# Two late tiles of the expert mixer are selected, and their gathers emitted, earlier in the dense stage

## The chip, the cores and the metric

The kernel runs on one core of one Trainium2 chip. The metric is device microseconds of one execution. Three runs of the kernel before gave 3964.43, 3979.69 and 3978.75 us, a median of 3978.75 us. One further execution was profiled. All times of stages and instructions below come from that one.

## The reference

The reference is one layer of a hybrid decoder: a norm, a joint input projection for two head groups, an output projection, the expert channel mixer, a per-layer input embedding and a final norm. It works on 1024 prompt rows and 64 sample rows of 1024 features. The change lies in the expert mixer, which in the reference reads:

```python
def peer(xn, wq, keys, u_tab, v_tab):
    ...
        q = (xb @ wq).reshape(PEER_BLOCK, PEER_HEADS, 2, PEER_DKEY // 2)
        s = jnp.einsum('phcd,hcnd->phcn', q, keys).astype(jnp.float32)
        sv, si = lax.top_k(s, PEER_TOPK)
        cand = sv[:, :, 0, :, None] + sv[:, :, 1, None, :]
        cv, ci = lax.top_k(cand.reshape(PEER_BLOCK, PEER_HEADS, PEER_TOPK * PEER_TOPK), PEER_TOPK)
        e = ...
        gsm = jax.nn.softmax(cv, axis=-1)
        hval = jnp.einsum('pd,phkd->phk', xb, u_tab[e])
        act = (jax.nn.gelu(hval.astype(jnp.float32), approximate=False) * gsm).astype(xb.dtype)
        return jnp.einsum('phk,phkd->pd', act, v_tab[e])
```

Each row picks 128 of 16384 experts (8 heads, 16 each), takes the product of its features with 128 rows of `u_tab`, and sums 128 weighted rows of `v_tab`.

## The kernel before

The rows are nine tiles: 0 to 7 hold 128 prompt rows each, tile 8 the 64 sample rows. The mixer is computed in two ways.

**Gathered tiles.** Tiles 0, 1, 8 (`E0`, during earlier stages) and 2, 3 (`G1`, the late tiles) fetch their own expert rows. `gather` issues 128 indirect DMAs of 128 x 1024 floats for `u_tab` and 128 more for `v_tab` on the queue of GpSimd (POOL). VectorE (DVE) works each one off with one `scalar_tensor_tensor`. Five buffers `grow` turn round, so the sixth DMA waits until DVE has used the first row. The two late tiles make 512 gathers.

**Dense tiles.** Tiles 4 to 7 (`G2`) are computed together against all experts, in 128 blocks of 128 experts:

- `hidden` multiplies one block of `u_tab` with the 512 rows (24 matmuls `ph`, since operands are split in a high and a low part: `uh` on ScalarE (ACT), `ul` on POOL).
- `gates` turns a tile's selection into weights for every expert and row. A tile takes 32 steps. A step is two comparisons `oh` on DVE, four scalings of `oh` on ACT, four matmuls `pwt` on TensorE (PE) and one copy `wst` on ACT. Ahead of its first step a tile's indices are transposed by three matmuls `pit`. After 16 steps four DMAs write the weights to `wd` in device memory.
- `act` reads weights back (`wt`), multiplies, and splits (`ah`, `al`). `dense` multiplies the result with `v_tab` (`py`, 24 matmuls a block; `vh` on ACT, `vl` on POOL).

Three stages follow one another. **Stage 1** (lines 1492 to 1513) loops over the four dense tiles and one last pass: top-k of a tile (DVE, some on POOL), the gate steps of the tile before, and a fifth of the first 96 `hidden` blocks, stored in `gd`. `TK1` says behind which pass a late tile's top-k and its whole gather are emitted. **Stage 2** (`dense_fused`) computes the last 32 blocks with `hidden` and `py` in turn; it needs every tile's weights. **Stage 3** (`dense_stored`) does `py` for the 96 stored blocks in groups of five, eight steps a group, and splits the weights of the embedding (`pga`, `pgb`, `pgx`) on the side. Then `ple` finishes all tiles, the late ones last.

The code emits the work in this order, but the framework's scheduler decides what each engine's queue holds: it orders the instructions of each engine by emission, readiness and its own clock. Each engine then runs its queue strictly in order. A gather that waits for a buffer on POOL so holds up an `ul` or `vl` behind it.

Of the kernel before, what the change touches and what calls it, by code (L numbers as in the profile page):

```python
# [166 lines left out]
PG = 0  # L167
PWS = 4
NPRE = 96
NF = 4  # L170
TK1 = {2: 1, 3: 4}
GEB = 2
GHB = 2
WQ = 32
# [5 lines left out]
G1 = [2, 3]  # L180
# [19 lines left out]
def spans(tiles):  # L200

    e = [sum(SIZE[t] for t in tiles[:i]) for i in range(len(tiles) + 1)]
    return dict(zip(tiles, e)), e[-1]
# [8 lines left out]
class K:  # L212
# [1204 lines left out]
    def build(self):  # L1417
        PS = bass.MemoryType.PSUM
        run = lambda g: [None for _ in g]
        sb = lambda name, es, **kw: self.pool(name, es=es, reuse_waits="tile", **kw)  # L1420
        with self.es:
            self.setup()
            em, ee, eg, et, ew, ex, ep, e0, e1, e2 = (ExitStack() for _ in range(10))
            acc = self.acc = self.pool("psumg", space=PS, es=eg, reuse_waits="tile")
            self.psums("psum", ep, a=2, b=3, d=1)
            self.rowed = set()
            pools = self.a_pool(e1, "1")
            mix = []

            def mixes():  # L1430
                self.setup_mix(em)
                mix.append(self.first_mix(e0))

            a = self.group_a(pools, A0, "b", mixes)
            while next(a) != "rw":
                pass
            m = mix[0]
            self.interleave(m, 1, a, IA)
            a = self.group_a(pools, A1, "b")
            self.interleave(m, IB, a, 1)  # L1440
            e1.close()
            e0.close()
            self.ep0 = ep0 = sb("early", ee, side="right")
            self.layout(ep0, [("V", [128, D], F32, ER), ("W", [128, D], F32, 1), ("xy", [128, D], F32, 1), ("Wq", [128, D], F32, 1), ("xT", [128, D], F32, 1)])
            early = self.behind(self.early(ep0), PE_)
            co = self.co = sb("co", ew, side="right")
            a = self.group_a(self.a_pool(e2, "2"), A2, "b")
            for _ in self.c_rows(co, E0[0]):
                next(a, None)
            for _ in a:  # L1450
                for _ in range(IE):
                    next(early, None)
            e2.close()
            late = self.group_b(BORDER, early)
            em.close()
            cq = sb("cq", ew, bufs=2, side="right")
            parts = [G1, G2]
            self.layout(cq, [(f"ss{g[0]}", [128, len(g), 2, 128], F32, 1) for g in parts] +
                        [(f"qT{g[0]}", [128, spans(g)[1]], F32, 1) for g in parts])
            cn = sb("cn", ew, side="right")  # L1460
            c1 = sb("cx1", ew, side="right")
            x1 = self.rows_of(c1, G1)
            cx = sb("cx2", ex)
            x = self.rows_of(cx, G2)
            da = sb("dna", eg, bufs=2)
            self.layout(da, [("uh", [128, 8, 128], F32R, DW), ("ul", [128, 8, 128], F32R, DW), ("uraw", [128, 8, 128], F32, UB)])
            tp = sb("tk", et)
            self.e12 = {}
            n3 = spans(G2[:-1])[1]
            query = self.c_query(cq, da, [(G1, x1), (G2, x)])  # L1470

            def rest():
                for t in late[:-1]:
                    yield from self.c_rows(co, t, CRING)

            run(self.rows_in(cn, G1, x1))
            run(rest())
            last = self.c_rows(co, late[-1], CRING, da, [y[:, :, n3:] for y in x])
            next(last)
            for _ in self.rows_in(cn, G2[:-1], x):  # L1480
                next(last, None)
            run(last)
            run(query)
            run(early)
            ew.close()
            ee.close()
            ep.close()
            self.group(G2)
            self.wd = self.dp.tile([self.ntok // 64, 128, 128, 64], F32, name="wd")
            self.gd = self.dp.tile([128, 128, self.ntok], F32, name="gd")  # L1490
            gp = sb("gat", eg, side="right")
            with ExitStack() as e:
                self.psums("psumw", e, i=1, w=2)
                self.psh = self.pool("psumh", bufs=3, space=PS, es=e, reuse_waits="tile")
                gw = sb("gw", e, side="right")
                self.layout(gw, [("oh0", [128, 4, 128], F32, 2), ("oh1", [128, 4, 128], F32, 2), ("it", [128, 128], F32, 2)])
                gh = sb("gh", e, bufs=2, side="right")
                gate = iter(())
                nh = 0
                for i, t in enumerate(G2 + [None]):  # L1500
                    tk = self.topk(tp, t) if t is not None else iter(())
                    while True:
                        a, b = next(tk, "end"), next(gate, "end")
                        if a == "end" and b == "end":
                            break
                    while nh < NPRE * (i + 1) // (len(G2) + 1):
                        self.nc.scalar.dma_start(self.gd[nh], self.hidden(da, gh, x, nh))
                        nh += 1
                    gate = self.gates(gw, t) if t is not None else gate
                    for t in G1:  # L1510
                        if i == TK1[t]:
                            run(self.topk(tp, t))
                            run(self.behind(self.gather(gp, t, acc=acc), PG))
            et.close()
            self.first = True
            with ExitStack() as e:
                dl = sb("dl", e, bufs=2)
                yT = sb("dy", e, side="right").tile([128, 8, self.ntok], F32, name="yT")
                with ExitStack() as e2:
                    self.ps2 = self.pool("psumy", bufs=3, space=PS, es=e2, reuse_waits="tile")  # L1520
                    self.psh = self.pool("psumh2", bufs=3, space=PS, es=e2, reuse_waits="tile")
                    dr = sb("dr", e2, bufs=2, side="right")
                    self.dense_fused(dl, dr, da, x, yT)
                    self.dense_stored(dl, dr, yT, self.ple_weights(cx, da, dl))
                self.psums("psum3", e, a=2, p=2)
                self.pst = self.pool("psumt", bufs=1, space=PS, es=e, reuse_waits="tile")
                self.ple(dl, sb("plt", e, bufs=2, side="right"), yT)
            eg.close()
            ex.close()
# [14 lines left out]
```

## Time and profile before

The profiled execution took 3954.93 us; its span, first to last instruction, is 3953.2 us. Engines run side by side, so busy times of different engines do not add up. In the page's groups a line stands with its engine, operation, output and input, count, busy time and mean.

| what | number |
|---|---|
| median of three runs | 3978.75 us |
| profiled execution, and its span | 3954.93 us, 3953.2 us |
| busy PE, DVE, POOL, ACT | 3349.9, 2957.2, 2322.7, 1222.2 us |
| moved by DMA | 1107.20 MB, of it 604.05 MB by gathers |
| first `ph` of stage 1 | 2093.9 us |
| first DVE instruction of the dense tiles' top-k | 2104.7 us |
| transposes `pit` of the last dense tile (7) | 2662.6 us |
| last `pwt` of tile 7 | about 2771 us |
| first gather of the late tiles | after 2358.7 us, where `eid` of tile 2 is written |

### The profile page before, as it was taken

To read this page: it belongs to the slowest core of one execution; us is meant where nothing else is said; L and a number is where in the kernel's file an instruction comes from. 1 tells how busy PE (TensorE), PEld (TensorE's weight loads), DVE (VectorE), ACT (ScalarE), POOL (GpSimd) and SP (SyncE) were. 2 spreads that over 40 slices of the span, in tenths; PEclk is the share of its full clock that TensorE was granted. 3 is DMA by queue.
4 is the path that set the end of the run, shared out by engine and by line. 5 is a ranking of instruction groups with operands and counts; after the bars stand their busy time and mean duration, and the time that the engine had idled before them with its cause. 6 is when DMAs were issued, how large, how long until landed. Compare 5 with 4: busy or idle time off the path is not lost. (4 is left out here: it accounts for less than half of the span.)

```text
span 3953.2 us, 52689 instructions
## 1 busy us (share of the span) xinstructions
PE 3349.9 (85%) x17749; PEld 2755.0 (70%) x17749; DVE 2957.2 (75%) x5764; ACT 1222.2 (31%) x2247; POOL 2322.7 (59%) x2051
## 2 busy tenths in 40 slices
PE   7789994865788585886699899999999989899989
PEld 7688993643566473665598677888788766677767
DVE  4454388978858879888857999986577777787775
ACT  4232221010022011111232466778332333333322
POOL 5253176555416656565544557775788777787740
PEclk9799995655698556887799999999999999999999
DMA  7266458989946998889974459888999999999962
GB/s 251 69 225 215 157 195 319 310 293 301 322 133 230 381 355 254 303 294 373 395 279 149 135 172 335 300 323 338 364 342 338 331 355 352 365 366 348 343 221 71
DMA packets 473864, 1107.20 MB, mean 280 GB/s; under 512 B 74555, under 2 KB 191545, under 8 KB 467642
## 3 DMA queue, kind: packets, MB, share of 16 engines
q0 software_dynamic: 165888, 604.05, 41.9%
q1 hardware_dynamic: 245694, 393.26, 30.7%
q10 hardware_dynamic: 62012, 106.52, 7.2%
q8 instruction: 141, 2.31, 0.2%
q14 instruction: 129, 1.06, 0.1%
HBM read 997.17 MB, written 106.43 MB: 279 GB/s over the span
## 5 line engine op out<-in xcount | busy, mean ns | idle before, releaser
L1127 POOL DMA_INDIRECT grow<-in_pv,eid x576 | 561.7, 975 | 382.9 <-DVE gacc L1155 221.6
L1127 POOL DMA_INDIRECT grow<-in_pu,eid x576 | 561.7, 975 | 343.9 <-DVE grow L1141 220.3
L1155 DVE SCALAR_TENSOR_TENSOR gacc<-grow,ac,gacc 128x1024 f32<-128x1024 f32 x571 | 732.4, 1283 | 36.8 <-DMA grow<-in_pv,eid 29.5
L1141 DVE SCALAR_TENSOR_TENSOR grow<-grow,gacc 128x1024 f32<-128x1024 f32 x576 | 686.7, 1212 | 63.5 <-DMA grow<-in_pu,eid 61.5
L1295 PE MATMUL py<-ah,vl 128*128 128x512 f32 x1024 | 410.1, 404 | 37.0 <-POOL vl L301 37.0
L1295 PE MATMUL py<-ah,vh 128*128 128x512 f32 x1024 | 407.0, 399 | 13.4 <-ACT vh L297 13.3
L326 PE MATMUL ph<-cx,uh 128*128 128x512 f32 x1024 | 408.2, 399 | 7.6 <-ACT uh L297 7.6
L328 PE MATMUL ph<-cx,ul 128*128 128x512 f32 x1024 | 407.5, 398 | 3.2 <-POOL ul L301 3.2
L1295 PE MATMUL py<-al,vh 128*128 128x512 f32 x1024 | 406.3, 397 | 0.0
L327 PE MATMUL ph<-cx,uh 128*128 128x512 f32 x1024 | 406.1, 397 | 0.0
L301 POOL TENSOR_TENSOR ul<-uraw,uh 128x1024 fp32r<-128x1024 f32 x128 | 308.2, 2409 | 152.8 <-ACT uh L297 150.8
L301 POOL TENSOR_TENSOR vl<-vraw,vh 128x640 fp32r<-128x640 f32 (+2 forms) x224 | 325.7, 1457 | 54.4 <-ACT vh L297 50.6
L297 ACT ACTIVATE vh<-vraw 128x640 fp32r<-128x640 f32 (+2 forms) x224 | 154.6, 692 | 382.7 <-PE py L1295 221.9
L1295 PEld LDWEIGHTS py<-ah,vl 128*128 128x128 f32 x1024 | 194.2, 190 | 102.6 <-POOL vl L301 60.9
L1299 DVE TENSOR_TENSOR yT<-yT,py 128x512 f32<-128x512 f32 x216 | 147.5, 684 | 143.7 <-PE py L1295 143.3
L1295 PEld LDWEIGHTS py<-ah,vh 128*128 128x128 f32 x1024 | 195.3, 191 | 65.9 <-ACT vh L297 24.7
L326 PEld LDWEIGHTS ph<-cx,uh 128*128 128x128 f32 x1024 | 195.5, 191 | 47.1 <-ACT uh L297 8.4
L328 PEld LDWEIGHTS ph<-cx,ul 128*128 128x128 f32 x1024 | 195.4, 191 | 43.9 <-POOL ul L301 4.3
L1295 PEld LDWEIGHTS py<-al,vh 128*128 128x128 f32 x1024 | 194.7, 190 | 44.4
L327 PEld LDWEIGHTS ph<-cx,uh 128*128 128x128 f32 x1024 | 195.4, 191 | 39.7
L1243 ACT ACTIVATE oh<-oh,it 128x128 f32<-128x128 f32 x512 | 161.8, 390 | 107.0 <-DVE oh L1241 96.2
L1241 DVE TENSOR_TENSOR oh<-csta,pit 128x512 f32<-128x512 f32 x256 | 161.5, 677 | 41.9 <-PE pwt L1246 41.9
(400 smaller groups left out, 7722.6 us busy)
## 6 DMA issues: line engine op xcount, KB each, us to landing
uraw<-in_puT SPq DMA_DIRECT2D x128, 512.0 KB, 4.5
vraw<-in_pvd SPq DMA_DIRECT2D x152, 320.0 KB, 5.8
cw<-in_w_out SPq DMA_DIRECT2D x128, 256.0 KB, 5.2
wd<-wst ACTq DMA_DIRECT2D x32, 1024.0 KB, 16.1
wt<-wd SPq DMA_DIRECT2D x64, 512.0 KB, 7.6
wraw<-in_w_ret SPq DMA_DIRECT2D x48, 512.0 KB, 4.9
ewq<-in_wq SPq DMA_DIRECT2D x48, 512.0 KB, 6.6
gd<-geh ACTq DMA_DIRECT2D x96, 256.0 KB, 4.5
```

The source lines that it names most:

```text
L297: nc.scalar.activation(hi, src, AF.Copy)
L301: nc.gpsimd.tensor_tensor(lo, src, hi.bitcast(F32), op=OP.subtract)
L326: mm(out, lh(k), rh(k), start=first and k == 0, stop=False)
L327: mm(out, lh(k), rl(k), start=False, stop=False)
L328: mm(out, ll(k), rh(k), start=False, stop=last and k == nk - 1)
L1127: nc.gpsimd.indirect_dma_start(out=g, out_offset=None, in_=src, in_offset=bass.IndirectOffsetOnAxis(ap=self.eid[t][:, j:j + 1], axis=0))
L1141: nc.vector.scalar_tensor_tensor(g[:, c], g[:, c], 1.0, x[:, c], op0=OP.mult, op1=OP.mult, accum_out=hv[:, i, j:j + 1])
L1155: nc.vector.scalar_tensor_tensor(y[:, c], g[:, c], ac[:, j:j + 1], y[:, c], op0=OP.mult, op1=OP.add)
L1241: nc.vector.tensor_tensor(oh[j], io, p[:, j, s + b:s + b + 4, None].to_broadcast([128, 4, 128]), op=OP.is_equal)
L1243: nc.scalar.activation(oh[0][:, j], oh[0][:, j], AF.Copy, scale=it[:, s + b + j:s + b + j + 1])
L1295: nc.tensor.matmul(p, lh[:, b, :], rh, start=b == 0 and j == 0, stop=b == nb - 1 and j == 2)
L1299: nc.vector.tensor_tensor(yT[:, d, :], yT[:, d, :], p, op=OP.add)
```

## The change

`TK1` goes from `{2: 1, 3: 4}` to `{2: -1, 3: 2}`: tile 2 is selected and its gather emitted ahead of the loop over the dense tiles (before: behind the second pass), tile 3 behind the third pass (before: behind the last). For the new place the two lines become an inner function.

```diff
-TK1 = {2: 1, 3: 4}
+TK1 = {2: -1, 3: 2}
...
+                def late_gather(i):
+                    for t in G1:
+                        if i == TK1[t]:
+                            run(self.topk(tp, t))
+                            run(self.behind(self.gather(gp, t, acc=acc), PG))
+
+                late_gather(-1)
                 for i, t in enumerate(G2 + [None]):
...
-                    for t in G1:
-                        if i == TK1[t]:
-                            run(self.topk(tp, t))
-                            run(self.behind(self.gather(gp, t, acc=acc), PG))
+                    late_gather(i)
```

No instruction of the computation is added or taken away; the queues are ordered differently. Counted over the queues from stage 1 on (a block is 24 matmuls, a gather one indirect DMA of the 512):

| place in the queue | before | changed |
|---|---|---|
| PE: blocks `ph` ahead of the `pit` of tiles 4, 5, 6, 7 | 19, 38.8, 58.8, 76 | 33.2, 60.5, 80.7, 98.1 |
| PE: blocks `ph` ahead of the last `pwt` of tile 7 | 89 | 99 |
| DVE: gathers ahead of the copy `it` of tile 7 (all six top-k done in both) | 91 | 181 |
| POOL: gathers ahead of the 64th `vl` (last of stage 2) | 286 | 359 |
| POOL: gathers ahead of the 144th `vl` (80 steps of stage 3) | 407 | 482 |
| POOL: the 512th gather stands behind | the last `vl` (224th) | the 167th `vl` |

PE, at the end of tile 7's gate steps. Each row is one or several matmuls: `pwt` of a gate step, `ph` of a hidden block, `py` of stage 2. Before:

```order
L328 MATMUL ph<-cx_13025,ul 128x512
L1246 MATMUL pwt<-oh_21886,oh_21887 128x128 x2
L326 MATMUL ph<-cx_13025,uh 128x512
L1246 MATMUL pwt<-oh_21886,oh_21887 128x128 x2
L327 MATMUL ph<-cx_13026,uh 128x512
L1246 MATMUL pwt<-oh_21900,oh_21901 128x128 x4
L328 MATMUL ph<-cx_13025,ul 128x512
```

The same place in the changed program:

```order
L1246 MATMUL pwt<-oh_22826,oh_22827 128x128 x4
L1246 MATMUL pwt<-oh_22840,oh_22841 128x128 x4
L1246 MATMUL pwt<-oh_22854,oh_22855 128x128 x4
L1246 MATMUL pwt<-oh_22868,oh_22869 128x128 x4
L1295 MATMUL py<-ah,vh 128x512 x2
L326 MATMUL ph<-cx_13025,uh 128x512
```

Before, the gate steps of tile 7 stand among 13 hidden blocks, and 9 more blocks follow ahead of the first `py`. Now 31 of the 32 steps stand in one piece, with no block between them, and the first `py` comes right behind them.

POOL, at the same place of the changed program (`ul` of the 103rd and 104th block, `vl` for stage 2, gathers of tile 2's `in_pv`):

```order
L301 TENSOR_TENSOR ul<-uraw,uh 128x1024
L1127 DMA grow<-in_pv,eid_67 128x1024 x20
L301 TENSOR_TENSOR vl<-vraw,vh 128x512 x2
L1127 DMA grow<-in_pv,eid_67 128x1024 x9
L301 TENSOR_TENSOR ul<-uraw,uh 128x1024
```

Before, one to three gathers stand between two splits there; now a run of 20 stands ahead of the first `vl` and 9 behind it.

POOL, at the end of stage 3 (the last `vl` of the stored blocks, and `nrs` of the embedding). Before:

```order
L301 TENSOR_TENSOR vl<-vraw,vh 128x128 x2
L1127 DMA grow<-in_pv,eid_68 128x1024 x2
L301 TENSOR_TENSOR vl<-vraw,vh 128x128 x3
L1127 DMA grow<-in_pv,eid_68 128x1024 x7
L291 TENSOR_SCALAR nrs<-nssq 128x1
```

The changed program:

```order
L301 TENSOR_TENSOR vl<-vraw,vh 128x640
L1127 DMA grow<-in_pv,eid_68 128x1024 x2
L301 TENSOR_TENSOR vl<-vraw,vh 128x640 x49
L301 TENSOR_TENSOR vl<-vraw,vh 128x128 x8
L291 TENSOR_SCALAR nrs<-nssq 128x1
```

Before, gathers stand between the splits up to the end, and ten stand behind the last one; now the last 57 splits have no gather among them or behind them.

## The prediction

> **What bounds the kernel now.** I read the page first, for the engines' totals:
>
> ```profile
> PE 3349.9 (85%) x17749; PEld 2755.0 (70%) x17749; DVE 2957.2 (75%) x5764; ACT 1222.2 (31%) x2247; POOL 2322.7 (59%) x2051
> q0 software_dynamic: 165888, 604.05, 41.9%
> L1127 POOL DMA_INDIRECT grow<-in_pv,eid x576 | 561.7, 975 | 382.9 <-DVE gacc L1155 221.6
> L1141 DVE SCALAR_TENSOR_TENSOR grow<-grow,gacc 128x1024 f32<-128x1024 f32 x576 | 686.7, 1212 | 63.5 <-DMA grow<-in_pu,eid 61.5
> ```
>
> PE is busiest, but the mean hides the stages. A gather moves 604.05 MB / 1152 = 0.524 MB and costs DVE 1.2 us. Next I cut the time from stage 1 on at points of the timeline (first block; first and last `pit`; last `pwt`; first `py`; first `py` of stage 3; half of it; its short last group; start of `ple`), and asked the windows view for busy times. The columns are PE, weight load, DVE, ACT, POOL, granted clock, DMA share, GB/s; the three rows below them are POOL's gathers alone in stage 3.
>
> ```profile
> 2094.00:2213.00 119.00, 105.46 (x458) 86.50 (x456) 106.34 (x582) 31.02 (x39) 60.47 (x41) 0.95 0.48 157
> 2213.00:2662.60 449.60, 421.54 (x2147) 355.40 (x2147) 415.50 (x1147) 307.41 (x609) 311.39 (x219) 0.96 0.73 260
> 2662.60:2771.00 108.40, 103.40 (x569) 89.36 (x568) 77.32 (x130) 84.57 (x185) 59.39 (x45) 0.98 0.90 336
> 2771.00:2832.00 61.00, 53.05 (x220) 42.95 (x220) 28.53 (x29) 16.96 (x23) 42.19 (x31) 0.92 1.01 380
> 2832.00:3178.00 346.00, 342.97 (x1490) 279.05 (x1489) 259.36 (x306) 111.38 (x171) 284.28 (x234) 1.00 0.97 340
> 3178.00:3508.00 330.00, 291.85 (x1159) 220.59 (x1160) 248.92 (x395) 118.51 (x193) 259.65 (x216) 0.96 1.01 357
> 3508.00:3774.00 266.00, 258.88 (x1105) 205.60 (x1104) 209.91 (x249) 97.28 (x156) 201.09 (x163) 1.00 0.98 344
> 3774.00:3805.00 31.00, 12.90 (x52) 8.39 (x50) 23.73 (x27) 4.45 (x12) 18.65 (x25) 0.78 0.96 339
> ```
>
> ```profile
> 3178.00:3508.00 330.00, 112.09 (x118) 0.96 1.01 357
> 3508.00:3774.00 266.00, 84.74 (x89) 1.00 0.98 344
> 3774.00:3805.00 31.00, 13.95 (x14) 0.78 0.96 339
> ```
>
> Stage 1 (2094 to 2771) is held by PE and DVE together: up to the last `pit` both are over 90% busy, while DMA has room (0.48, 0.73). Stage 2 is PE alone (343 of 346 us). Stage 3 is DMA and POOL in its first half (DMA share 1.01, PE 292 of 330 us), nearly PE in its second. PE's own waits there say through whom DMA works:
>
> ```profile
> PE py L1295 <- POOL vl L301: 35.0, 40, 2.0
> PE py L1295 <- ACT vh L297: 11.6, 21, 4.1
> ```
>
> The `vl` that PE waits for stand behind gathers in POOL's queue. So the idea of the change has ground: gathers leave a crowded stage for one with DMA to spare. What it costs is the order in stage 1.
>
> **The change part by part.** No work is added, so each term is a shift of PE idle time. The unit is a block of 24 matmuls, from the chain of waits in stage 2:
>
> ```profile
> 2969.97 5.53 PE py L1295 x24
> ```
>
> *(a) Later arrival at tile 7's gate steps.* PE's queue now holds 98.1 blocks ahead of tile 7's `pit`, before 76. That is 22.1 x 5.53 = **+122 us**; the 384 other `pwt` stand ahead of it in both. DVE gives a second estimate: 181 gathers instead of 91 ahead of its copy `it`, 90 x 1.21 = +109 us, all else equal. Both engines were over 90% busy, so neither shift finds a hole; I take the larger. If they add in part it is up to 25 us more. Ahead of it tile 2's top-k stands in front of tile 4's, but 14 more blocks now cover that wait. Tile 2's first gathers fall ahead of 2358.7 us, where no late gather ran before, and SP's block loads pass nothing that waits longer.
>
> *(b) The gate steps run bare.* Before, tile 7's 32 steps took 108.4 us (third row of the table) with 13 blocks between them. Now one block stands at their start and 31 steps follow alone. PE takes 1.78 us for two steps (first row, the chain of waits), so ACT sets the pace (three rows of ACT's timeline):
>
> ```profile
> 2762.37 1.78 PE pwt L1246 x16
> ```
>
> ```profile
> 2712.13 1.28 ACT L1243 ACTIVATE oh<-oh,it 128x128 f32<-128x128 f32 x4
> 2713.30 1.13 ACT L1247 ACTIVATE wst<-pwt 128x512 f32<-128x512 f32 x1
> 2714.19 1.26 ACT L1243 ACTIVATE oh<-oh,it 128x128 f32<-128x128 f32 x4
> ```
>
> From one group of scalings to the next are 2714.19 - 2712.13 = 2.06 us. 31 steps are 64 us, the block 5: 69 us, or **-39 us** against 108.4. The other end: if steps keep their old pace of 108.4 / 32 = 3.4 us, 31 take 105 us and the term is about 0.
>
> *(c) Nothing covers the weights' way through memory.* Ahead of the first `py` the last half tile of weights must be written, read back, multiplied and split. The rows are from the chain of waits, the DMA view of 2760 to 2840, and the groups of 2771 to 2900:
>
> ```profile
> 2774.46 19.04 DMA wd<-wst
> ```
>
> ```profile
> wt<-wd SPq DMA_DIRECT2D x3, 512.0 KB, 11.1
> ```
>
> ```profile
> L1274 DVE TENSOR_TENSOR ph<-ph,wt 128x512 f32<-128x512 f32 x9 | 6.3, 698 | 12.4 <-ACT ph L1263 12.3
> L297 ACT ACTIVATE ah<-ph 128x512 fp32r<-128x512 f32 x9 | 5.4, 596 | 5.4 <-DVE ph L1274 5.4
> ```
>
> The write lands at 2793.5, 22.5 us behind the last `pwt` (2771). The read takes 11.1, multiply and split 1.3: 35 us. Before, nine blocks hid it all but 61 - 53 = 8 us. Now `py` comes right behind `pwt`, and PE waits it out. It then starts slowly, as it did after a pause of a few us:
>
> ```profile
> 2800.00:2804.00 4.00, 2.60 (x5) 0.50 1.09 378
> 2804.00:2808.00 4.00, 4.00 (x11) 0.50 1.04 399
> ```
>
> Seven us at half clock lose 3.5. The term is 35 + 3.5 - 8 = **+30 us**. With the page's medians (wd 16.1, wt 7.6) it is 18; with ten us more in a crowd of gathers, 40.
>
> ```profile
> wd<-wst ACTq DMA_DIRECT2D x32, 1024.0 KB, 16.1
> wt<-wd SPq DMA_DIRECT2D x64, 512.0 KB, 7.6
> ```
>
> The Trainium skill, page "TensorE: Matmul & The Clock Gate", section "HAM oscillation — how this bites in real kernels", asks for no PE pause longer than about 3.4 us, and so speaks against this change. The two rows at 0.50 agree for the restart. Were its half clock to hold through the bare steps too, `pwt` would take twice 0.89 us a step and still hide behind ACT; chained behind it, the sum comes out as in the rival "slow steps" below.
>
> *(d) Blocks in hand.* At the last `pwt` 99 blocks are done, before 89: 10 x 5.53 = **-55 us** in what is left of stage 2, which is PE alone and has the same gathers as before.
>
> Stages 1 and 2 together: 122 - 39 + 30 - 55 = +58 us.
>
> *(e) Stage 3.* POOL has 153 gathers left at its start, before 226. But the queue fixes where they stand: in the first 80 steps 123 gathers, before 121, so this half stays at 330 us and loses some 3 us (2 x 0.524 MB at 357 GB/s). In the next 24 steps the density is as before. Only the last 48 full steps and the short group are free. The second half's 72 full steps took 266 us, 3.69 each; PE's 15 matmuls need 15/24 x 5.53 = 3.46, so 48 steps give back 11 us at most: **-11 us** (the other end 0). So nearly all of the relief falls where PE had little to wait for.
>
> *(f) The tail.* The short group and the wait for `ple` took 31 us with PE busy 12.9:
>
> ```profile
> 3805.11 1.11 PE L320 MATMUL ntr<-csta,njunk 128*128 128x128 f32 x4 [14.65 <-DVE njunk L311]
> ```
>
> Gathers between its splits slow the group (16 us for eight steps; I take 8), and DVE's last gathers stand ahead of `ple`'s first addition (of the wait of 14.65 I take off 6). **-14 us**; ends -5 and -20.
>
> The sum is 58 + 3 - 11 - 14 = **+36 us**. On the profiled execution's 3954.93 us that is 3991 us. That execution lies 0.6% under the median of 3978.75 us, so I add to the median: **4015 us**, slower by 0.9%. A measurement of this kernel can tell about 0.5%, 20 us, from no change.
>
> **The rivals.**
>
> *Slow steps.* The bare steps take 3.4 us instead of 2.06: DVE's comparisons share its queue with 19 gathers there, each of which can wait for its DMA, and PE, mostly idle, runs at half clock. For: steps in before did take 3.4. Against: then ACT and PE had blocks to work on. Sum +36 + 36 = +72 us, 4051 us.
>
> *A wash.* DVE's 109 us is the true shift of (a), the weights' way takes the page's medians (term 18): 109 - 39 + 18 - 55 = +33, and stage 3 with its tail gives back 22. Sum +11, 3990 us. For: PE's 449.6 us ahead of `pit` held some 28 us of idle time. Against: DVE had no more of it.
>
> *DMA relief in full, the other side: faster.* If stage 3 is paced by bytes as a whole, not by the place of each gather in POOL's queue, 73 fewer gathers (38 MB at 351 GB/s, 109 us) count up to PE's floor: 2304 matmuls are 96 x 5.53 = 531 us, with 13 us for the tail 544 instead of 627, -83. Sum 58 - 83 = -25, 3954 us. It decides if the first 80 steps take under 280 us instead of 330. For: the DMA share of 1.01. Against: the same 123 gathers stand between the same 80 `vl`. The Trainium skill, page "DMA: Bandwidth & Descriptors", section "Issuing engines are not separate DMA queues", says that transfers of SP, ACT and POOL share the same 16 DMA engines, whoever issues them; by that alone, the bytes taken out would come back as time. The shares of 0.97 to 1.01 with gathers and loads together agree.
>
> *The change does nothing it says.* The first gathers could be held by something else in stage 1. The queue speaks against it: the late tile's index is written ahead of tile 4's. 3979 us.
>
> **How the numbers follow.** Forecast 0.41, slow steps 0.22, a wash 0.25, faster 0.10, no effect 0.02. Slower by over 0.5%: slow steps 0.22 and most of the forecast 0.36, in all 0.58. Faster by over 0.5%: the last rival and the edge of the wash, 0.12. The rest, 0.30, lies within. The range takes in the wash with its low ends (about -20, 3960 us) and slow steps with ten us more for the weights' way and some for (a) (+85, 4064 us); it leaves out the faster rival and the far upper edge.
>
> **What would show it.** In the changed profile: tile 7's `pit` near 2662.6 + 122 = 2785 us, not before 2770 (a); 31 steps of `pwt` without `ph`, over 64 to 105 us, PE about 40% busy (b); a PE pause near 35 us that ends with `wt` and `ah`, clock 0.50 behind it (c); stage 3 beginning near 3178 + 58 = 3236 us; 80 steps in about 330 us, then steps near 3.5 us with no wait for `vl` (e); a pause ahead of `ple` under 10 us (f). I am wrong if `pit` comes by 2740, if blocks fill the gate steps after all, or if the first 80 steps fall to 280 us.

## The result, and the profile after

The changed kernel takes **4013.29 us** (median of four runs, 4010.9 to 4024.18). The kernel before takes 3972.6 us beside it (median of four runs, 3964.43 to 3979.69). The ratio is 1.0111, with a 95% interval of 1.009 to 1.0132: slower by 1.1%, 40.7 us. Forecast were 4015 us and +36 us. The total was hit more closely than the terms deserve: the base of 3978.75 us lay 6 us above this median, and the difference came out 5 us larger than forecast.

The profiled execution of the changed kernel took 4024.18 us (span 4022.4), 69 us more than that of before. Half of this is no effect of the change: the first `ph` of stage 1 comes at 2128.9 us, before at 2093.9, and the queues up to there are the same. Over all profiled executions of this study it came between 2093.9 and 2129.7 us, in no order by kernel. So all times below are counted from each execution's own first `ph`; "+" marks them. By this count the program ends at +1893.5 us, before at +1859.3: **34.2 us** later. The medians say 40.7; the 6.5 us between the two belong to no stage that I could find.

The totals on the page of the changed kernel:

```profile
PE 3387.4 (84%) x17749; PEld 2788.9 (69%) x17749; DVE 2978.6 (74%) x5764; ACT 1226.4 (30%) x2247; POOL 2327.8 (58%) x2051
q0 software_dynamic: 165888, 604.05, 41.6%
L1141 DVE SCALAR_TENSOR_TENSOR grow<-grow,gacc 128x1024 f32<-128x1024 f32 x576 | 684.9, 1212 | 37.0 <-DMA grow<-in_pu,eid 26.7
L1295 PE MATMUL py<-ah,vh 128*128 128x512 f32 x1024 | 407.2, 398 | 38.6 <-ACT ah L297 25.9
```

Counts and bytes are the old ones, and so are the means of a gather's work. PE's busy time is 37.5 us more for the same 17749 instructions, but 29.2 of it lie ahead of the first `ph` (1650.2 us against 1621.0), where the change does nothing. From there on it is 8 us. The last row has a new wait, 25.9 us for `ah`.

The timeline of the changed kernel, cut at the same points as before (first block; last `pit`; last `pwt`; first `py`; first `py` of stage 3; 80 steps; 24 steps; last full step; start of `ple`), in the windows view. Columns are PE, weight load, DVE, ACT, POOL, granted clock, DMA share, GB/s. The cuts at 80 and 104 steps lie up to 4 us late. The second fence has POOL's gathers alone, in the stretches of stage 3.

```profile
2129.00:2820.20 691.20, 648.25 (x3138) 539.57 (x3136) 649.50 (x1855) 375.70 (x694) 518.06 (x373) 0.98 0.83 290
2820.20:2901.50 81.30, 54.14 (x280) 48.53 (x277) 67.21 (x88) 68.45 (x163) 25.78 (x25) 0.80 0.77 286
2901.50:2927.70 26.20, 0.29 (x3) 0.03 (x1) 12.46 (x12) 2.86 (x5) 9.07 (x9) 0.50 0.92 340
2927.70:3271.20 343.50, 338.30 (x1464) 275.68 (x1464) 262.54 (x389) 108.05 (x167) 281.42 (x236) 0.99 0.98 349
3271.20:3607.20 336.00, 301.67 (x1216) 229.87 (x1217) 261.14 (x330) 124.29 (x201) 270.63 (x225) 0.97 1.02 367
3607.20:3690.20 83.00, 82.00 (x352) 65.26 (x351) 66.24 (x80) 32.05 (x52) 62.45 (x51) 1.00 1.01 355
3690.20:3857.20 167.00, 166.37 (x717) 133.79 (x716) 68.85 (x102) 61.43 (x98) 74.01 (x48) 1.00 0.55 164
3857.20:3874.60 17.40, 6.87 (x34) 5.02 (x32) 9.46 (x13) 4.07 (x11) 4.02 (x9) 0.76 0.71 233
```

```profile
3271.20:3607.20 336.00, 117.60 (x124) 0.97 1.02 367
3607.20:3690.20 83.00, 25.64 (x27) 1.00 1.01 355
3690.20:3857.20 167.00, 0.00 (x0) 1.00 0.55 164
```

Four things are to be seen. Stage 1 is as full as before but 122 us longer up to tile 7's `pit` (first row). Then PE is busy two thirds of 81 us, at a clock of 0.80, and not at all for 26 us. Stage 3's first 80 steps keep their gathers (124 in that row, at a DMA share of 1.02) and take nearly as long as before. And where the gathers are gone, DMA has room (share 0.55, 164 GB/s) beside a PE that is busy 166.37 of 167 us and has nothing to gain from it.

| stage | before | changed | difference |
|---|---|---|---|
| first `ph` to the last `pit` of tile 7 | 568.7 | 691.1 | +122.4 |
| to the last `pwt` | 108.5 | 81.3 | -27.2 |
| to the first `py` | 61.2 | 26.4 | -34.8 |
| to the first `py` of stage 3 | 348.5 | 343.5 | -5.0 |
| to the end of the last full step of stage 3 | 597.5 | 586.0 | -11.5 |
| to the first `ntr` of `ple` | 26.8 | 17.4 | -9.4 |
| to the end | 148.1 | 147.8 | -0.3 |

Before, the last full step ends at 3778.4 us. The prediction's table cuts at 3774, 18 matmuls earlier, and so counts 4 us of full steps as tail.

### The profile page after: what moved, and what is told of

It reads as the page before. It is cut to its first block, busy times and chain, and to the rows that moved or that the text cites. A ratio compares the mean times of both kernels' runs of the same rounds, so it can differ in the third digit from the quotient of the medians.

```text
span 4022.4 us, 52688 instructions
## 1 busy us (share of the span) xinstructions
PE 3387.4 (84%) x17749; PEld 2788.9 (69%) x17749; DVE 2978.6 (74%) x5764; ACT 1226.4 (30%) x2247; POOL 2327.8 (58%) x2051
## 4 chain that ended last, share of the span: by engine, by line
PE 30%; DVE 14%; DMA 5%; issue 4%; POOL 4%; ACT 2%; ACTq 0%; another core or an unknown queue 0%; POOLq 0%; DVEq 0%; SPq 0%
PE py L1295 13%; DVE grow L1141 3%; PE ph L326 2%; PE ph L328 2%; PE ph L327 2%; POOL grow L1127 1%; PE pwt L1246 1%; POOL vl L301 1%; DVE oh L1241 1%; DVE eq L1082 1%; DMA vraw<-in_pvd 1%; DVE gacc L1155 1%; PE pq L326 1%; PE pq L327 1%; PE pq L328 1%
## 5 line engine op out<-in xcount | busy, mean ns | idle before, releaser
L1155 DVE SCALAR_TENSOR_TENSOR gacc<-grow,ac,gacc 128x1024 f32<-128x1024 f32 x571 | 732.8, 1283 | 38.2 <-DMA grow<-in_pv,eid 30.5
L1295 PE MATMUL py<-ah,vh 128*128 128x512 f32 x1024 | 407.2, 398 | 38.6 <-ACT ah L297 25.9
L1295 PEld LDWEIGHTS py<-ah,vh 128*128 128x128 f32 x1024 | 194.8, 190 | 88.9 <-ACT ah L297 26.2
L297 ACT ACTIVATE uh<-uraw 128x1024 fp32r<-128x1024 f32 x128 | 135.4, 1058 | 276.5 <-DMA uraw<-in_puT 124.2
L1246 PE MATMUL pwt<-oh,oh 128*128 128x128 f32 x1024 | 155.7, 304 | 53.8 <-ACT oh L1243 45.8
```

The costliest lines, as they stand in the source:

```text
L297: nc.scalar.activation(hi, src, AF.Copy)
L1155: nc.vector.scalar_tensor_tensor(y[:, c], g[:, c], ac[:, j:j + 1], y[:, c], op0=OP.mult, op1=OP.add)
L1246: nc.tensor.matmul(pw[:, j, :], oh[1][:, j, :], oh[0][:, j, :], start=True, stop=True)
L1295: nc.tensor.matmul(p, lh[:, b, :], rh, start=b == 0 and j == 0, stop=b == nb - 1 and j == 2)
```

## The experiments

Their expectations name these theories. **Q** (the prediction's own): PE's queue loses blocks to the front of stage 1, so tile 7's gate steps and the weights' way through memory run bare. **T3**: tile 3's place does it. **C**: the moved gathers crowd stage 1, whatever blocks remain. **B**: stage 3's first 80 steps are paced by the bytes that stand between them; **W**: only by where a `vl` stands behind a gather.

One row for each run; the times come from its profile, counted from its first `ph`.

| run | blocks ahead of `pit` | `pit` | last `pwt` | first `py` | end | ratio (95%) |
|---|---|---|---|---|---|---|
| before | 76 | 568.7 | 677.2 | 738.4 | 1859.3 | |
| the change | 98.1 | 691.1 | 772.4 | 798.8 | 1893.5 | 1.0111 (1.009 to 1.0132) |
| tile 2 moved alone | 96 | 676.7 | 759.8 | 786.0 | 1882.6 | 1.0074 (1.0045 to 1.0104) |
| tile 3 moved alone | 76.2 | 569.3 | 681.5 | 741.2 | 1860.5 | 1.001 (0.9994 to 1.0026) |
| the change, 112 blocks | 97.8 | 690.3 | 809.8 | 838.8 | 1858.7 | 0.9989 (0.9972 to 1.0006) |
| before, 112 blocks | 88 | 631.6 | 741.4 | 824.2 | 1858.4 | 1.0000 (0.9982 to 1.0019) |
| tile 2 behind the first pass | 82.2 | 599.2 | 722.2 | 752.5 | 1861.0 | 0.9999 (0.9979 to 1.0018) |
| the change, side work spread | 98.1 | 689.0 | 768.9 | 795.2 | 1885.5 | 1.0061 (1.004 to 1.0081) |
| before, side work spread | 76 | 567.3 | 676.5 | 737.4 | 1853.4 | 0.9989 (0.9971 to 1.0006) |
| the change, 112 blocks, spread | 97.8 | 689.1 | 809.4 | 837.9 | 1869.4 | 1.0026 (1.0006 to 1.0045) |
| the change, 104 blocks | 97.8 | 688.7 | 796.6 | 823.4 | 1872.0 | 1.0034 (1.0017 to 1.0051) |
| tile 2 behind the first pass, spread | 82.2 | 598.7 | 721.5 | 751.6 | 1860.9 | 1.0008 (0.9996 to 1.002) |
| the same, 104 blocks | 83 | 602.3 | 718.1 | 787.9 | 1856.5 | 0.9983 (0.9968 to 0.9998) |

**Which half of the change?** Tile 2 alone, and tile 3 alone:

```diff
-TK1 = {2: -1, 3: 2}
+TK1 = {2: -1, 3: 4}
```

> Tile 2 moved as in the change, tile 3 where it was before (TK1 2: -1, 3: 4). Theory Q (queue): the loss comes from tile 2's gathers in stage 1, which delay tile 7's gate steps until PE's 99 blocks are used up; then 31 steps and the weights' way stand bare. PE's queue here has 96 blocks ahead of tile 7's pit and 99 ahead of its last pwt and of the first py, nearly as in the change: ratio to before 1.008 to 1.013, a pause of 25 us or more ahead of the first py. Rival T3: it is tile 3's top-k and gather behind the third pass that cost; then the ratio is 0.997 to 1.003.

```diff
-TK1 = {2: -1, 3: 2}
+TK1 = {2: 1, 3: 2}
```

> Tile 3 moved as in the change, tile 2 where it was before (TK1 2: 1, 3: 2). Q: PE's queue is that of before (76 blocks ahead of tile 7's pit, 90 ahead of its last pwt), so nothing changes: ratio 0.997 to 1.003. Rival T3: 1.006 or more.

Tile 2 in front of the loop brings two thirds of the loss (1.0074, a little under the 1.008 expected); its bare steps (83.1 us) and its idle time (26.2) are those of the change. Tile 3 alone does nothing that can be measured (1.001). Together they lose 11 us more than tile 2 alone, 14 of them ahead of `pit`, of which 3 come back. T3 falls as a cause by itself.

**Fill the bare stretch.** `NPRE` says how many blocks are stored in stage 1. With 112 instead of 96 the queue holds 15 blocks among tile 7's gate steps and 2 behind them, and the gathers stay in front. The same number in the kernel before is the control.

```diff
-NPRE = 96
+NPRE = 112
```

> The change with 112 instead of 96 blocks stored in stage 1 (NPRE). PE's queue then has 97.8 blocks ahead of tile 7's pit, 112.9 ahead of the last pwt, 115 ahead of the first py. Q: blocks fill the gate steps again. Steps 82 -> about 109 us (+27), the pause of 26 us loses 10 of it to two blocks, blocks in hand 99 -> 113 (-77): stages 1 and 2 become 60 us shorter than in the change; 16 more blocks through memory (8.4 MB) cost 10 to 30 us in stages 1 and 3. Ratio to before 0.994 to 1.004. Rival C (crowding): the gathers slow PE's blocks in stage 1 through DMA and POOL, wherever they stand; more traffic there makes it worse: ratio 1.010 or more.

> The kernel before with 112 stored blocks: the control of e3. Q: before had blocks enough for its gate steps and lost only 8 us ahead of the first py, so the extra blocks buy at most 8 us and cost up to 24 us (8.4 MB at 354 GB/s): ratio 0.998 to 1.006. If 112 blocks are simply better, whatever the gathers do, e4 gains as much as e3 does against the change (1% or more).

The loss is gone (0.9989), and the control gains nothing (1.0000). The windows view of the change with 112 blocks: gate steps, then the time up to the first `py`.

```profile
2807.30:2926.80 119.50, 113.92 (x622) 97.84 (x620) 86.24 (x102) 88.81 (x191) 67.96 (x51) 1.00 0.90 336
2926.80:2955.80 29.00, 11.68 (x53) 9.35 (x52) 12.92 (x13) 7.50 (x11) 14.70 (x12) 0.75 0.97 377
```

PE is busy 114 of 119.5 us, at full clock. Fourteen more blocks, 14 x 5.53 = 77 us of work, made the steps only 119.5 - 81.3 = 38 us longer: the other 39 us are what the bare steps waste. The gathers are as early as in the change and `pit` as late (+690.3), so C is refuted.

**Half the dose.** With 104 blocks, 9 stand among the steps and none behind them.

```diff
-NPRE = 96
+NPRE = 104
```

> The change with 104 stored blocks. By the queue, 9 blocks stand among tile 7's gate steps (1 with 96 blocks, 15 with 112), and none between the last step and the first py, as in the change. It fills half of the bare steps and leaves the weights' way bare. Theory Q, in which a block that fits into a bare step is free: transposes of tile 7 at first ph + 690, steps about 103 (81.3 and 119.5 on either side), idle time ahead of the first py about 26 still; 8 blocks (44) more done for 22 of time: some 20 less than the change, ratio 1.004 to 1.007. Rival (the bare weights' way makes the loss, the steps do not): ratio 1.010 to 1.012, as the change.

The windows view of this run, at the same two places:

```profile
2786.50:2894.40 107.90, 92.41 (x480) 79.74 (x479) 76.73 (x95) 81.79 (x182) 54.13 (x41) 0.91 0.83 313
2894.40:2921.20 26.80, 0.43 (x3) 0.14 (x1) 14.35 (x13) 2.79 (x5) 10.08 (x11) 0.50 0.94 349
```

The weights' way is as bare as in the change (26.8 us, PE 0.43), and yet two thirds of the loss are gone: 1.0034, a little better than the 1.004 expected. So the steps weigh more than the weights' way.

**Another place for tile 2.** Behind the first pass it takes only 6.2 blocks to the front instead of 20.

```diff
-TK1 = {2: -1, 3: 2}
+TK1 = {2: 0, 3: 4}
```

> Tile 2 goes behind the first pass (-1 in the change, 1 before), tile 3 behind the last as before. By the queue, 82 blocks then stand ahead of tile 7's transposes (before 76, the change 98), 15 stand among its gate steps (before 13, the change 1) and 2 behind them (before 9, the change 0). Theory Q (a block that stands early is missing where PE waits later): transposes of tile 7 at first ph + 603 (569 before + 6.2 x 5.53), steps about 110 as before, so nothing is lost there, and only the weights' way is bare: about 26 of idle time, of which two blocks hide 11. Start of stage 3 some 15 to 20 us later than before, half of it back by the end: ratio 1.001 to 1.005. Rival (any load of gathers in the first pass costs, whatever the blocks do): as tile 2 alone in front of the loop, ratio 1.007.

Measured 0.9999, just below the expected 1.001. The windows view of this run:

```profile
2716.00:2839.00 123.00, 115.39 (x613) 98.73 (x612) 85.97 (x109) 88.18 (x189) 67.43 (x52) 0.97 0.88 328
2839.00:2869.30 30.30, 11.44 (x53) 9.18 (x51) 13.01 (x13) 8.41 (x12) 16.19 (x14) 0.74 0.99 374
```

The steps are covered, and the weights' way is not (19 of 30 us idle). Stage 3 begins 12.5 us later than before (15 to 20 expected), and the program ends 1.7 us later: here the gathers that left stage 3 pay for the idle time. Earlier gathers by themselves do not cost.

**What paces stage 3?** `PWS` sets how many steps lie between two weight splits of the embedding. At 7 instead of 4 they take 140 steps instead of 80. First on the change, then on the kernel before:

```diff
-PWS = 4
+PWS = 7
```

> The change with the embedding's weight splits spread over 140 steps of stage 3 instead of 80 (PWS 7 for 4); stages 1 and 2 have the same order on PE. Theory B (the first 80 steps are paced by the bytes and gathers that stand between them): 111 gathers instead of 123 stand there, and 3/7 of the side loads leave, so they take about 310 us instead of 336, while the next 60 steps go from 3.45 to about 3.6 us; in all 10 to 20 us less than the change: ratio against before 1.006 to 1.009. Rival W (only the place of vl behind a gather counts, not how many): stage 3 as in the change, 603 us, ratio 1.011.

> The kernel before with the embedding's weight splits spread over 140 steps instead of 80. There is no free stretch behind the 80 steps here, since gathers stand between all steps to the end. Theory B: the first 80 steps have 114 gathers instead of 121 and fewer side loads, 338 falls to about 318, and the 60 next steps get the same bytes back at 3.53 a step: near no change, ratio 0.996 to 1.001. If spreading the side work helped by itself, it would be 0.99.

B holds on the change (1.0061). First the changed kernel: the transfers of its first 80 steps, from the DMA view, and the windows view of the same stretch for the matmuls of `py` alone.

```profile
DMA packets 65549, 123.20 MB, mean 367 GB/s; under 512 B 4791, under 2 KB 30391, under 8 KB 65527
```

```profile
3271.20:3607.20 336.00, 301.67 (x1216) 0.97 1.02 367
```

Then the same two views of the change with the side work spread:

```profile
DMA packets 61962, 112.91 MB, mean 363 GB/s; under 512 B 4398, under 2 KB 29968, under 8 KB 61942
```

```profile
3269.80:3580.80 311.00, 291.48 (x1202) 0.99 1.01 363
```

For 1200 matmuls (80 steps) that is 331.6 us with 121.6 MB against 310.5 us with 112.7 MB. The 8.9 MB less, at 365 GB/s, are 24 us; 21 were gained. So the work that stands between the steps paces this half, not the mere place of a `vl`. That it is the bytes of this work is likely and not shown apart: DMA keeps its share (1.02, 1.01) and its rate in both, while POOL is busy 81% and 79% of the 80 steps; but POOL's busy time fell by 22 us too (268.0 to 246.1). The steps behind them pay most of it back (81st to 140th step: 3.80 us each instead of 3.53), and the program ends 8 us earlier. On the kernel before the same edit ends 6 us earlier, 0.9989, no difference that can be told.

**Combinations, in search of a version faster than both.** The change with 112 blocks and `PWS` 8:

```diff
-PWS = 4
-NPRE = 96
+PWS = 8
+NPRE = 112
```

> The change with 112 instead of 96 stored blocks and the side splits spread over 160 steps. Stages 1 and 2 as with 112 blocks alone (ratio 0.9989). Theory B: 110 instead of 113 gathers and half the side loads in the first 80 steps, which become 15 to 25 us shorter; the freed stretch at the end takes the rest: ratio 0.992 to 0.996, faster than both kernels. Rival W: 0.999.

A miss: 1.0026. The first 80 steps did become 17 us shorter (319.5 us against 336.3), as expected, but the next 72 became 25 us longer (286.7 against 262.1), and stage 3 is 9 us longer than with 112 blocks alone. DMA moved 353 GB/s in its first 616 us, there 359, and PE waited 16.1 us for `vh` instead of 9.7; why the rate fell was not tried. Tile 2 behind the first pass with `PWS` 7, and the same with 104 blocks:

```diff
-TK1 = {2: -1, 3: 2}
-PWS = 4
+TK1 = {2: 0, 3: 4}
+PWS = 7
```

> Tile 2 behind the first pass, tile 3 as before, and the embedding's splits spread over 140 steps. Stage 1 and 2 as in the run with tile 2 behind the first pass (no loss against before), the first 80 steps of stage 3 about 15 shorter by the bytes that leave them, the next 60 some 10 longer: ratio 0.996 to 0.9995. Rival: as with 112 blocks, the spread work costs more behind the 80 steps than it frees among them: ratio 1.001 to 1.003.

> The same with 104 stored blocks, so that eight blocks more (10 instead of 2) stand between the last gate step of tile 7 and the first py and cover the weights' way (about 20 of idle time). If idle time of PE there is what is left of the loss, 0.992 to 0.996, faster than both kernels; if stage 3's bytes take it back, 0.997 to 1.000.

The first misses too (1.0008): the first 80 steps became 18 us shorter, as expected, and the next 60 became 23 us longer instead of 10 (241.1 against 218.1, at a DMA share of 0.99 in both). Bytes that leave the first half for steps in which DMA is as full only move. The second is at 0.9983, the best of all, but 0.17% is less than the 0.5% that a measurement here can tell. Its ten blocks covered less than I thought: PE still waits 11.0 us for `uh` and 4.6 for `ul` there, in place of 18.7 for `ah`. No version clearly beats the kernel before.

## Why the prediction was right, step by step

*(a) Later arrival: +122 forecast, +122.4 measured.* PE's count was the right measure: of the 122.4 us PE was busy 121 more, and its idle time in the stretch stayed at 42 to 43 us. With tile 2 alone 20 more blocks should be 110.6 us and were 108.0; with tile 2 behind the first pass 6.2 blocks should be 34.3 and were 30.5; the control with 12 more blocks should be 66 and was 62.9. PE's count never misses by over 4 us. DVE's second estimate (+109) is too low for the change, and the control decides between the two: its trace has 115 gathers ahead of the copy `it` instead of 91, which would make only 24 x 1.21 = 29 us of the 62.9.

*(b) Bare steps: -39 forecast, -27.2 measured.* The order was as read (31 steps in a piece), and ACT's pace was right where the clock was full. Two stretches of the chain of waits in the changed kernel:

```profile
2882.28 1.04 ACT oh L1243 x4
2883.32 0.93 ACT wst L1247
2884.25 1.04 ACT oh L1243 x4
...
2896.10 0.17 ACT oh L1243
2896.31 2.09 PE pwt L1246 x8
2898.43 1.04 ACT wst L1247
2899.47 0.18 ACT oh L1243
2899.69 2.09 PE pwt L1246 x8
```

In the upper three rows a step is 2884.25 - 2882.28 = 1.97 us, ACT alone (2.06 forecast). In the lower ones it is 2899.69 - 2896.31 = 3.38 us: at half clock PE's own 2.09 stand in the loop, since `wst` waits for `pwt` and the next `pwt` for an `oh` behind that `wst` in ACT's queue. The windows view of these steps, `pwt` alone (PE's busy time, clock, DMA share, GB/s):

```profile
2834.00:2836.00 2.00, 0.20 (x2) 0.83 1.01 418
2836.00:2842.00 6.00, 5.21 (x24) 0.50 1.02 420
2842.00:2848.00 6.00, 4.23 (x26) 0.99 0.82 333
2868.00:2876.00 8.00, 6.71 (x31) 0.50 1.01 412
2880.00:2888.00 8.00, 5.46 (x32) 1.00 0.14 58
2893.00:2901.50 8.50, 5.91 (x26) 0.52 0.75 216
```

The clock flips between 1.00 and 0.50 several times. The prediction's aside that `pwt` at half clock would "still hide behind ACT" was wrong; it priced that chained case in the rival "slow steps", at 3.4 us for every step. The truth lies between: 76.4 us for 31 steps, 2.46 each, so +12 on this term, with PE about 64% busy instead of 40%.

Half clock is one part of it. 31 x 1.97 = 61 us would have been ACT's pace, so 15 us are to be explained, and PE's three longest pauses in these steps have other sources. In the first (2.68 us, shown in the last section) ACT had a split `uh`, a block's `ph` and two copies `wst` ahead of its scalings; the row names a `gacc` of DVE, which ended at the same moment as the first scaling. In the second (2.59 us, shown there too) DVE's comparisons stood in the queue behind a `gacc` that waited for a gather. The third stands between the half tiles, where ACT issues the four DMAs that write the weights; the sum had left them out. The second in the chain of waits, and the third in PE's timeline:

```profile
2820.77 13.30 DMA grow<-in_pv,eid
2834.17 0.06 DVE gacc L1155
```

```profile
2867.23 3.78 PE L1246 MATMUL pwt<-oh,oh 128*128 128x128 f32 x16 [4.32 <-ACT oh L1243]
```

Beyond the usual pause of 0.6 us the three make 7.8 us, by this estimate about half of the 15; the rest is left for the half clock. Both reasons that the rival "slow steps" gave were there, the wait for a gather once.

*(c) The weights' way: +30 forecast, about +20 measured.* The mechanism is there piece by piece. The chain of waits in the changed kernel, behind the last `wst`:

```profile
2905.24 16.61 DMA wd<-wst
2921.94 4.33 DMA wt<-wd
2926.29 0.71 DVE ph L1274
2927.03 0.60 ACT ah L297
2927.68 1.22 PE py L1295 x2
```

The write lands at 2921.85, 20 us behind the last `pwt` (22.5 forecast). The read took 4.33 us, not 11.1: that was the sum's oversized piece. Multiply and split take 1.3 as forecast. PE's pause is 25.9 us instead of 35. (The low end, by the medians of the profile's page, was put at 18; its own pieces, 3.5 ahead of the write, 16.1, 7.6, 1.3 and 3.5, less 8, make 24.) It restarts at half clock for 3.3 us (up to 2931), which loses 1.7, not 3.5.

*(d) Blocks in hand: -55 forecast.* With (c) at +20 the two rows of the table (-34.8 and -5.0) leave -60. The errors of (b), (c) and (d), +12, -10 and -5, cancel: stages 1 and 2 cost +55.4, forecast +58. Right as a sum, by terms that were right in kind, two of them off by a third in size; that their errors cancel is luck.

*(e) Stage 3: -8 forecast, -11.5 measured.* The windows that the sum used were not quite the steps: 1159 matmuls in 330 us are 77 steps, not 80, and 1105 in 266 us nearly 74, not 72. Cut at the matmuls themselves (ends of the 80th, 104th and 152nd step), `py` alone, before and then changed (busy time, clock, DMA share, GB/s):

```profile
3180.76:3517.57 336.81, 301.41 (x1201) 0.96 1.01 358
3517.57:3605.88 88.31, 84.93 (x361) 1.00 1.00 357
3605.88:3778.36 172.48, 168.75 (x721) 1.00 0.96 333
```

```profile
3271.20:3603.58 332.38, 298.05 (x1201) 0.97 1.02 367
3603.58:3688.91 85.33, 84.33 (x361) 1.00 1.01 355
3688.91:3857.11 168.20, 167.57 (x722) 1.00 0.56 164
```

The first 80 steps fell by 4.4 us instead of rising by 3, and the next 24 by 3.0 instead of nothing. The last 48, the only ones that are free of gathers now, gave back 4.3 us and not 11: they had taken 3.59 us a step, not 3.69, and take 3.50 now, near the floor of 3.46. So the relief was even smaller than forecast where it was looked for. The 4.4 us of the first half need no cause in the change: with tile 3 moved alone, where the same 121 gathers stand between these steps as before, they took 331.9 us. The reason given, that each gather's place in POOL's queue fixes what is left in the first half, holds: 122 gathers stand between the first 80 steps, before 121. Through what it works was not quite as told: with the side work spread the half gave way with the work between its steps.

*(f) The tail: -14 forecast, -9.4 measured.* PE's waits in stage 3 of the changed kernel:

```profile
PE py L1295 <- POOL vl L301: 27.3, 33, 2.0
PE ntr L320 <- DVE njunk L311: 10.0, 1, 10.0
```

The wait ahead of `ple` is 10.0 us; 6 off 14.65 was near, if not under 10 as the text had it. The short group took 6.3 us instead of 9.9. The 16 us of the sum held 4 us of full steps, so the 8 us that it took off were too many. (e) and (f) together are -20.9, forecast -22: again a sum that is better than its terms.

**The rivals.** *Slow steps* held for part of the steps only. *A wash* needed 109 for (a) and 18 for (c). (c) was nearly so, and (a) was not; its argument that DVE had no more idle time than PE's 28 us was misread (449.6 - 415.5 = 34). *DMA relief in full* would have shown 80 steps under 280 us: they took 332. It had the wrong place: the first half is paced by the work that stands between its steps, most likely by the bytes, but what the change took away stood behind it, where PE is near its floor. *Nothing it says* is refuted by `pit` alone.

On the cause, the runs show that blocks missing from the gate steps make most of the loss: filling them ends it, half a fill ends two thirds of it, and leaving them there avoids it. How the rest splits between the weights' way and stage 3 is only worked out from the terms. The change with 112 blocks is no faster than the control with as many (+1858.7 and +1858.4), although its gathers are done earlier. Their traces say where the gain goes: the change begins stage 3 12.3 us later, its first 152 steps take 598.4 us against 596.5, since gathers stand among them in both, and only behind them, where the control still has 52 gathers and the change 4, does it get 13.8 us back.

## What to carry to other kernels

Work of an engine that waits for nobody is also cover for later chains that wait for somebody: before moving other work in front, count how many independent blocks still stand among the chain's steps in that engine's queue, since such a block costs its full time up front and only part of it there (here 38 of 77 us for fourteen blocks). A transfer taken off a saturated stretch pays only if it leaves the steps that DMA paces. Read where in the queue it stood, and ask what else holds the stretch that is freed: beside an engine at its floor, idle bandwidth is worth nothing.

## What the runs showed of the hardware

The clock fell sooner than I had expected. PE's timeline in the changed kernel, at two of the bare steps; the bracket is the pause ahead of them, and what ended it by the profile:

```profile
2829.69 2.53 PE L1246 MATMUL pwt<-oh,oh 128*128 128x128 f32 x16 [2.68 <-DVE gacc L1155]
...
2836.79 6.71 PE L1246 MATMUL pwt<-oh,oh 128*128 128x128 f32 x32 [2.59 <-ACT oh L1243]
```

In the rows of (b) the clock is 0.83 from 2834 to 2836 us, so it fell while the second pause still lasted, then 0.50 for six us, then 0.99. The Trainium skill, page "TensorE: Matmul & The Clock Gate", section "HAM oscillation — how this bites in real kernels", puts the bound for such pauses at about 3.4 us; here the clock fell with none longer than 2.68 us in the ten us before. Later it fell with less. The windows view of `pwt` between the last two rows of (b) (busy time, clock, DMA share, GB/s), and the longest pause in that time:

```profile
2888.00:2893.00 5.00, 2.65 (x16) 1.00 0.69 210
```

```profile
2891.91 3.11 PE L1246 MATMUL pwt<-oh,oh 128*128 128x128 f32 x16 [1.30 <-ACT oh L1243]
```

From 2880 to 2888 us, steps with pauses of 0.6 us kept the full clock, and PE was busy 68% of the time. From 2888 to 2893 it was busy 53%, and at the end of that the clock fell, though no pause in either row exceeded 1.3 us. At half clock, steps with pauses of 1.3 us did not bring it back (2893 to 2901.5, 0.52). So the length of a single pause does not tell the clock in a chain of small matmuls; that the busy share does is a guess from these rows.
